# Two transformer blocks with a 16-of-16384 expert layer: decode of expert indices moved to GpSimd and ScalarE, order of work beside the gathers changed

## The chip, the cores and the metric

The kernel runs on one core of a Trainium2 chip. Its engines are TensorE (PE), VectorE (DVE), ScalarE (ACT), GpSimd (POOL) and SyncE (SP); each works through its own queue in order. The metric is the device time of one execution in microseconds, and less is better. Three timed runs of the kernel before took 2024.09, 2025.24 and 2026.83 us, median 2025.24.

## What is computed

x has 256 tokens of 1024 features. A first block (gated linear attention, a spatial gating unit, then the expert layer below) is followed by two layers of a second block, in which x attends to itself and to a second stream, ctx, of 256 tokens. ctx itself goes through attention and a gated FFN only in the first of these layers. The parts that the change touches:

```python
def peer(h, w_q, keys1, keys2, expert_down, expert_up):     # 8 heads, top 16 of 128 x 128 experts
    q = einsum('btd,dq->btq', h, w_q).reshape(B, T, 8, 2, 128)
    s1, s2 = q[..., 0, :] @ keys1.T, q[..., 1, :] @ keys2.T
    v1, i1 = top_k(s1, 16); v2, i2 = top_k(s2, 16)
    cand = v1[..., :, None] + v2[..., None, :]              # 16 x 16 sums
    cidx = i1[..., :, None] * 128 + i2[..., None, :]
    top_s, pos = top_k(cand.reshape(..., 256), 16)
    idx = take_along_axis(cidx.reshape(..., 256), pos)      # rows of the tables
    g = softmax(top_s)
    a = gelu(einsum('pd,ped->pe', h, expert_down[idx]))     # 128 rows of 1024 a token
    return einsum('pe,ped->pd', g * a, expert_up[idx])

# ctx in the first layer of the second block
o = softmax(q @ k.T * scale) @ v                            # three kinds of heads, 20 maps of 256 x 256 in all
y = (silu(h @ w_gate) * (h @ w_up)) @ w_down                # hidden width 2816 = 22 x 128
```

## The kernel before, in words

Tokens lie on the 128 partitions, in two halves t = 0 and 1. The program is written with a scheduler that orders each engine's instructions by its own model of their times, within the dependences and the extra edges that the code gives: `issue_after(ins)` puts what is traced inside it behind `ins` on the same engine. `merge` and `slow` interleave generators by the numbers that they yield, so a `yield 1.46` is meant as 1.46 us of the stage's time, and the order of writing is the scheduler's priority.

**The expert stage** (`experts`, L764) makes four passes of 128 rows. A row is one expert of each of 128 tokens, 128 x 1024 floats or 512 KiB, gathered by an indirect DMA that GpSimd issues (`gather`, L875) into a ring of 7 buffers. *Dot* passes multiply the row with h on DVE and add up (`dot_slot`, L859, instruction at L862); *up* passes add weight times row into a sum (L793, L795). h in the dot passes and the sum in the up passes lie in one PSUM tile, `side` (called h2p in the rows). The passes run dot and up for t = 0, then dot and up for t = 1; here they are called dot 0, up 0, dot 1 and up 1.

**The search** for one head and half (`winners`, L825) is some 25 short instructions on DVE: two top-16 searches over 128 scores (`top16`), the 256 sums `cand`, a top-16 over them, then the decode: the positions are split in two numbers by shift and mask (`pp`), cast on ScalarE (`ppf`, `vif`), compared with 0 to 15 to a one-hot `oh` (L849), multiplied with the found indices (L852), summed (L854) and put together to `idx` (L855). Heads of t = 0 are searched beside dot 0, one step after each row; those of t = 1 are written two steps a row from row 60 of up 0 on (`SECOND_AT`, `behind`). Between a dot and an up pass stand the softmax of the 8 heads' scores (`softmax_gate`), a gelu over all 128 dots on ScalarE (L784) and a product on DVE (L785).

**ctx's first layer** runs beside the expert stage, slowed by `CTX_SLOW` = 1.4. Its softmax (L1173) takes one score map at a time: matmul into PSUM, maximum on DVE (`sst`, L1180), exponential with its sum on ScalarE (L1182). Its norms (`norm_T`) scale the rows on DVE (L371). Its FFN goes through 22 feature tiles of 128: two weight loads and 16 matmuls into `gu`, tanh on ScalarE (L1404), two products on DVE (`fth`, L1405, and `hid`, L1413), a third load and four matmuls with `hid`, and the generator yields 6.8 and 3.4 a tile. Weight loads go out on SP's queue into four buffers `raw`; all other DMA of the stage is the gathers.

After the stage the two layers of x run alone, bound by TensorE and its operands; the ctx stream's key and value part of the second layer lies among them.

Of the kernel before, what the change touches and what calls it, by code (L numbers as in the profile page):

```python
# [20 lines left out]
P = 128  # L21
# [88 lines left out]
class Kern:  # L110
# [653 lines left out]
    def experts(self, A):  # L764

        nc, a, dot = self.nc, self.a, self.dot
# [8 lines left out]
        for t in range(2):  # L775
            for h in range(8):
                ahead = self.winners(A, h + 1, 0) if t == 0 and h < 7 else iter(())
                for n in range(16):
                    self.dot_slot(t, h * 16 + n)
                    next(ahead, None)  # L780
                    yield 1.46
                drain(ahead)
            self.softmax_gate(A, t)
            nc.scalar.activation(dot[:, t, :], dot[:, t, :], AF.Gelu)  # L784
            nc.vector.tensor_mul(dot[:, t, :], dot[:, t, :], self.gate[:, t].rearrange("p a b -> p (a b)"))  # L785
            y2 = side
            for s in range(P):
                if s >= SECOND_AT:
                    self.behind(second, 2)
                r = self.gather(a["up"], t, s)  # L790
                w = dot[:, t, s:s + 1]
                if s == 0:
                    self.slot = nc.vector.tensor_scalar(y2, r, w, None, op0=ALU.mult)  # L793
                else:
                    self.slot = nc.vector.scalar_tensor_tensor(y2, r, w, y2, op0=ALU.mult, op1=ALU.add)  # L795
# [3 lines left out]
            nc.vector.tensor_mul(g, y2, self.gate2)  # L799
# [25 lines left out]
    def winners(self, A, h, t):  # L825
# [4 lines left out]
        for f in range(2):  # L830
# [28 lines left out]
    def dot_slot(self, t, s):  # L859
# [3 lines left out]
                                       accum_out=self.dot[:, t, s:s + 1])  # L863
# [320 lines left out]

    def scale_rows(self, x, r, st, i):
# [16 lines left out]
    def attn_diff(self, st, l, W, kvs, dd):  # L1202
# [28 lines left out]
    def attn_pair(self, st, W, yT, tile_i, qf, kf, vf, kvs):  # L1231
# [87 lines left out]
    def layer(self, st, l, W, K, only_kv=False):  # L1319
# [56 lines left out]
        with ExitStack() as fs:  # L1376
# [14 lines left out]
            for ft in range(NFT):  # L1391
                if split and ft == GVFT:
                    gv = self.bcast_row(self.scratch(), cc[:, 3, :])
                with self.pinned(norm_ins):
                    self.upto(vec, VN)
# [8 lines left out]
                nc.scalar.activation(th, ps[:, 0, :], AF.Tanh, scale=0.5)  # L1404
                nc.vector.scalar_tensor_tensor(th, th, 1.0, ps[:, 0, :], op0=ALU.add, op1=ALU.mult)  # L1405
# [8 lines left out]
                yield 5.1 if split else 6.8  # L1414
# [8 lines left out]
                products(0)  # L1423
                later.append(products)
# [9 lines left out]
                yield 2.6 if split else 3.4  # L1434
# [20 lines left out]
    def run(self):  # L1455
# [10 lines left out]
        with ExitStack() as cs:  # L1466
# [9 lines left out]
            self.dot = self.ring.tile([P, 2, P], F32, name="dot", bufs=1)  # L1476
# [11 lines left out]
            merge(self.experts(A), slow(ctx_gen(), CTX_SLOW))  # L1488
# [126 lines left out]
SECOND_AT = 60  # L1615
# [37 lines left out]
```

## Time and profile before

| quantity | value |
|---|---|
| median of three runs | 2025.24 us |
| profiled execution, its own time | 2027.85 us |
| its span | 2026.1 us |
| PE / DVE / ACT / POOL busy, share of the span | 75% / 71% / 33% / 28% |
| DMA moved | 542.33 MB, mean 268 GB/s |
| expert stage, first to last row instruction's pass end | 357.0 to 1218.7 us |
| mean granted TensorE clock | 0.876 |

The page divides the span in 40 slices of 50.65 us. The shares of the whole span say little, since the stages have different limits: up to about 350 us the first block runs on TensorE, from 1219 us on the two layers of x do, and in between lie the 512 gathered rows. So the reading goes by stretches of the expert stage, its waits, and the groups of instructions that the change removes or adds. "Idle before" of a group is the time in which the engine stood still just before its instructions, with what ended it.

### The profile page before, as it was taken

How to read it: one execution, taken by the hardware profiler on the slowest of the kernel's cores; microseconds unless marked ns; L12 is line 12 of the kernel's file. 1: busy time of each engine (PE TensorE's matmuls, PEld its weight loads, DVE VectorE, ACT ScalarE, POOL GpSimd, SP SyncE). 2: the span in 40 equal slices, each digit the busy share in tenths (PEclk: the TensorE clock that was granted, in tenths of full speed). 3: DMA queues.
4: the chain of work that ended last, by engine and by line, in shares of the span. 5: the costliest groups of instructions: out<-in, count | busy, mean ns of one | idle time of the engine just before them, and what ended most of it. 6: DMA issues, size and time to landing. Idle time of an engine off the chain costs nothing.

```text
span 2026.1 us, 23153 instructions
## 1 busy us (share of the span) xinstructions
PE 1526.6 (75%) x7984; PEld 1153.7 (57%) x7984; DVE 1447.7 (71%) x2591; ACT 666.7 (33%) x1286; POOL 565.9 (28%) x596
## 2 busy tenths in 40 slices
PE   5999999995477877877000007789999988889997
PEld 1766666843344655554000006577988966769997
DVE  2444544999978799867999996664877557745554
ACT  2533333232242000000000006565544356755443
POOL 0000001555655444545776760300000004000000
PEclk9999999997568999988555558989999998899999
DMA  8867796998979999999999993423887543025652
GB/s 317 328 218 261 242 348 248 332 398 317 351 284 375 408 344 331 397 394 389 409 401 380 409 384 112 164 85 97 306 275 266 167 140 112 1 66 185 187 186 94
DMA packets 150184, 542.33 MB, mean 268 GB/s; under 512 B 16801, under 2 KB 17185, under 8 KB 150066
## 3 DMA queue, kind: packets, MB, share of 16 engines
q1 hardware_dynamic: 75152, 269.53, 38.3%
q0 software_dynamic: 73728, 268.47, 34.8%
q10 hardware_dynamic: 1186, 2.85, 0.4%
q8 instruction: 63, 1.03, 0.2%
q14 instruction: 55, 0.45, 0.1%
HBM read 539.73 MB, written 1.05 MB: 267 GB/s over the span
## 4 chain that ended last, share of the span: by engine, by line
PE 48%; DVE 24%; issue 9%; POOL 9%; DMA 8%; ACT 2%; POOLq 0%; SPq 0%; DVEq 0%; ACTq 0%
PE blk L206 14%; PE gu L206 12%; POOL row L878 7%; DVE row L862 7%; PE f L206 6%; DVE h2p L795 6%; PE ada L255 3%; DMA raw<-in_w_ada 2%; PE S L206 2%; DMA row<-in_up,idx 2%; PE po L1250 2%; PE PT L1196 2%; DMA vraw<-in_w_ada 2%; DMA araw<-in_w_ada 1%; PE qk L206 1%
## 5 line engine op out<-in xcount | busy, mean ns | idle before, releaser
L190 DVE TENSOR_TENSOR wlo<-raw,whi 128x1024 fp32r<-128x1024 f32 (+1 forms) x245 | 297.5, 1220 | 272.0 <-ACT whi L188 264.0
L188 ACT CAST whi<-raw 128x1024 fp32r<-128x1024 f32 (+1 forms) x245 | 254.3, 1043 | 329.6 <-PE blk L206 112.9
L795 DVE SCALAR_TENSOR_TENSOR h2p<-row,dot,h2p 128x1024 f32<-128x1024 f32 x254 | 326.8, 1286 | 17.4 <-DMA row<-in_up,idx 11.4
L862 DVE SCALAR_TENSOR_TENSOR row<-row,h2p 128x1024 f32<-128x1024 f32 x256 | 306.6, 1220 | 14.3 <-DMA row<-in_down,idx 11.5
L878 POOL DMA_INDIRECT row<-in_down,idx x256 | 245.5, 959 | 197.2 <-DVE row L862 118.5
L878 POOL DMA_INDIRECT row<-in_up,idx x256 | 243.1, 949 | 187.9 <-DVE h2p L795 103.3
L379 PE MATMUL nT<-cst,w 128*128 128x128 f32 x112 | 20.5, 341 | 293.8 <-DVE ss L305 270.6
L307 POOL TENSOR_TENSOR ss<-ss,mhalf 128x1 f32<-128x1 f32 (+1 forms) x39 | 25.4, 655 | 711.8 <-DVE ss L305 709.7
L206 PE MATMUL gu<-bTh,whi 128*128 128x256 f32 x704 | 201.0, 286 | 3.3 <-ACT bTh L352 2.8
L206 PE MATMUL gu<-bTl,whi 128*128 128x256 f32 x704 | 201.0, 285 | 0.7 <-DVE bTl L357 0.7
L206 PE MATMUL gu<-bTh,wlo 128*128 128x256 f32 x704 | 200.6, 285 | 0.1
L379 PEld LDWEIGHTS nT<-cst,w 128*128 128x128 f32 x112 | 16.4, 175 | 299.3 <-ACT junk L326 271.4
L206 PE MATMUL gu<-bT,raw 128*128 128x256 f32 x704 | 157.0, 381 | 0.7 <-DMA raw<-in_wgu 0.7
L206 PEld LDWEIGHTS gu<-bT,raw 128*128 128x128 f32 x704 | 134.6, 191 | 28.7 <-issue 10.4
L206 PEld LDWEIGHTS gu<-bTh,whi 128*128 128x128 f32 x704 | 135.9, 193 | 6.2 <-ACT bTh L352 3.4
L206 PEld LDWEIGHTS gu<-bTl,whi 128*128 128x128 f32 x704 | 136.0, 193 | 3.1 <-DVE bTl L357 1.5
L206 PEld LDWEIGHTS gu<-bTh,wlo 128*128 128x128 f32 x704 | 136.0, 193 | 1.6 <-DVE wlo L190 0.3
L206 PE MATMUL f<-raw,hid 128*128 128x512 f32 x176 | 93.2, 679 | 55.4 <-DVE hid L1413 51.6
L206 PEld LDWEIGHTS f<-raw,hid 128*128 128x128 f32 x176 | 36.1, 216 | 102.4 <-DVE hid L1413 63.8
L1180 DVE TENSOR_REDUCE sst<-S 128x1 f32<-128x512 f32 (+1 forms) x120 | 70.4, 601 | 32.4 <-PE S L206 31.5
L206 PE MATMUL blk<-wlo,hTh 128*128 128x512 f32 x224 | 90.8, 405 | 0.0
L206 PE MATMUL blk<-whi,hTl 128*128 128x512 f32 x224 | 88.1, 396 | 0.0
(406 smaller groups left out, 3102.0 us busy)
## 6 DMA issues: line engine op xcount, KB each, us to landing
raw<-in_wgu SPq DMA_DIRECT2D x132, 512.0 KB, 4.6
araw<-in_w_ada SPq DMA_DIRECT2D x72, 512.0 KB, 6.1
raw<-in_wd SPq DMA_DIRECT2D x66, 512.0 KB, 5.0
raw<-in_w1b SPq DMA_DIRECT2D x56, 512.0 KB, 5.1
raw<-in_w_ada SPq DMA_DIRECT2D x40, 512.0 KB, 4.4
vraw<-in_w_ada SPq DMA_DIRECT2D x32, 512.0 KB, 5.2
raw<-in_w2c SPq DMA_DIRECT2D x24, 512.0 KB, 4.8
raw<-in_w2o SPq DMA_DIRECT2D x24, 512.0 KB, 4.0
```

The costliest lines, as they stand in the source:

```text
L188: nc.scalar.copy(hi[:, :n], raw[:, :n])
L190: nc.vector.tensor_sub(lo[:, :n], raw[:, :n], hi[:, :n].bitcast(F32))
L206: self.mm_last = self.nc.tensor.matmul(out, l, r, start=first and i == 0, stop=last and i == n - 1)
L255: mm = nc.tensor.matmul(ps[32 * j:32 * j + 32, :], lhs[:, k, :], raws[j // 2][:, j % 2 * 512:(j % 2 + 1) * 512], start=k == 0, stop=k == K ...
L307: nc.gpsimd.tensor_tensor(ss, ss, self.mhalf[:, :n], op=ALU.pow)
L379: nc.tensor.transpose(ps[:, q, t * P:(t + 1) * P], xn[t][:, k * P:(k + 1) * P], self.ident)
L795: self.slot = nc.vector.scalar_tensor_tensor(y2, r, w, y2, op0=ALU.mult, op1=ALU.add)
L862: self.slot = nc.vector.scalar_tensor_tensor(r, r, 1.0, self.side, op0=ALU.mult, op1=ALU.mult, accum_out=self.dot[:, t, s:s + 1])
L878: nc.gpsimd.indirect_dma_start(out=r, out_offset=None, in_=table, in_offset=bass.IndirectOffsetOnAxis(ap=self.idx[:, t, s:s + 1], axis=0))
L1180: nc.vector.tensor_reduce(st[:, 0:1], ps, axis=AX.X, op=ALU.max, negate=True)
L1196: nc.tensor.transpose(ps[:, j, :], pr[:, j * P:(j + 1) * P], self.ident)
L1250: nc.tensor.matmul(po[64 * i:64 * i + 64, :], vf(kvs[j // 2], j % 2, i), PTs[i][:, j, :], start=j == 0, stop=j == 2 * nk - 1)
```

## The change

- **Decode.** For every head but the first of t = 0, the one-hot is made without DVE: GpSimd subtracts, ScalarE takes Abs and then Relu(1 - x), GpSimd multiplies. DVE keeps the sum and the last step. `winners` gets three more steps.
- **Searches of t = 1.** One step behind two of every three rows, from row 1 of up 0, instead of two steps behind each row from row 60. What is left is written after the pass.
- **Gelu in two parts.** The dots lie in tiles of 96 and 32 (`FIRST`); the first is weighed at row 116 of the dot pass, the second at row 4 of the up pass, and the softmax over heads' scores is written before the eighth head's rows.
- **ctx's softmax in pairs.** Where there is one key source, two score maps share a PSUM tile and one maximum instruction of 128x2x256; a yield of `CTX_LAG` = 2.0 stands before what uses them.
- **ctx's FFN.** The gate and up products of a tile are written before the DVE products of the tile ahead of it, and the yields are 9.0 and 5.6 a tile (x 1.4 = 20.4, that is 14 rows of 1.46).
- **ctx's norms** scale on ScalarE. All of ctx's generator is pinned behind the latest row instruction (`rows_first`).

```diff
+            if len(op) == 2:
+                self.xn_ins = nc.vector.tensor_scalar(j, x[:, t, :], r, None, op0=ALU.mult)
+            else:
+                nc.scalar.activation(j, x[:, t, :], AF.Copy, scale=r)
...
+                if h == 7:
+                    self.softmax_gate(A, t)
                 for n in range(16):
                     self.dot_slot(t, h * 16 + n)
                     next(ahead, None)
+                    if h * 16 + n == FIRST + 20:
+                        self.weigh(t, 0)
...
             for s in range(P):
-                if s >= SECOND_AT:
-                    self.behind(second, 2)
+                if t == 0 and s % 3:
+                    self.behind(second, 1)
...
+                if s == 4:
+                    self.weigh(t, 1)
...
+    def rows_first(self, g):
+        while True:
+            with self.pinned(self.slot):
+                y = next(g, None)
...
+        if h == 0 and t == 0:
+            nc.vector.tensor_tensor(oh, pb, ib, op=ALU.is_equal)
+            nc.vector.tensor_tensor(oh, oh, vb, op=ALU.mult)
+        else:
+            yield
+            nc.gpsimd.tensor_tensor(oh, pb, ib, op=ALU.subtract)
+            nc.scalar.activation(oh, oh, AF.Abs)
+            nc.scalar.activation(oh, oh, AF.Relu, scale=-1.0, bias=1.0)
+            yield
+            yield
+            nc.gpsimd.tensor_tensor(oh, oh, vb, op=ALU.mult)
...
+    def softmax2(self, W, pairs):
+        ps = self._ps(self.acc, [P, 2, T], "acc", "S")
+        for i, (lhs, kT) in enumerate(pairs):
+            self.mm(ps[:, i, :], self.pairs(lhs, kT), True, True)
+        nc.vector.tensor_reduce(st[:, 0:2], ps, axis=AX.X, op=ALU.max, negate=True)
+        for i in range(2):
+            nc.scalar.activation(pr[i], ps[:, i, :], AF.Exp, bias=st[:, i:i + 1], accum_out=st[:, 2 + i:3 + i])
...
+                for ft in range(NFT + 1):
+                    this = front(ft) if ft < NFT else None
+                    yield FRONT
+                    if ahead is not None:
+                        down(ft - 1, hidden(*ahead))(1)
+                        yield BACK
+                    ahead = this
...
+            self.slot = None
+            merge(self.experts(A), slow(self.rows_first(ctx_gen()), CTX_SLOW))
...
-SECOND_AT = 60
+FIRST = 96
+CTX_LAG = 2.0
+FRONT = 9.0
+BACK = 5.6
```

What the built programs show, at three places. GpSimd at the start of dot 0, before (`DMA row` is a gather, `ss` a norm's power function):

```order
L878 DMA row<-in_down,idx 128x1024 x2
L307 TENSOR_TENSOR ss_2702<-ss_2702,mhalf 128x1
L307 TENSOR_TENSOR ss_2709<-ss_2709,mhalf 128x1
L878 DMA row<-in_down,idx 128x1024 x42
L307 TENSOR_TENSOR ss<-ss,mhalf 128x2
```

and after:

```order
L916 DMA row<-in_down,idx 128x1024 x8
L884 TENSOR_TENSOR oh<-ppf,iota 128x512
L916 DMA row<-in_down,idx 128x1024 x2
L889 TENSOR_TENSOR oh<-oh,vif 128x512
L916 DMA row<-in_down,idx 128x1024 x6
L884 TENSOR_TENSOR oh<-ppf,iota 128x512
L916 DMA row<-in_down,idx 128x1024
```

The decode's difference and product now stand in the gathers' queue, one or two gathers apart, at 15 places of the stage.

ScalarE in up 0, where the FFN's tanh (`fth`) and the decode's casts meet, before:

```order
L1404 ACTIVATE fth<-gu 128x256 x4
L845 CAST vif<-tvi 128x32
L1404 ACTIVATE fth<-gu 128x256
L844 CAST ppf<-pp 128x32
L845 CAST vif<-tvi 128x32
```

and after:

```order
L1468 ACTIVATE fth<-gu 128x256
L870 CAST ppf<-pp 128x32
L1468 ACTIVATE fth<-gu 128x256
L885 ACTIVATE oh<-oh 128x512
L886 ACTIVATE oh<-oh 128x512
L1468 ACTIVATE fth<-gu 128x256
L871 CAST vif<-tvi 128x32
```

Abs and Relu (L885, L886) stand behind a tanh in this queue; the row shown is the first head of t = 1 that meets the FFN.

DVE where feature tiles pass among rows, before (up 0):

```order
L1405 SCALAR_TENSOR_TENSOR fth<-fth,gu 128x256
L1413 SCALAR_TENSOR_TENSOR hid<-fth,gu 128x256
L795 SCALAR_TENSOR_TENSOR h2p<-row,dot,h2p 128x1024 x6
L1405 SCALAR_TENSOR_TENSOR fth<-fth,gu 128x256
L1413 SCALAR_TENSOR_TENSOR hid<-fth,gu 128x256
```

and after (dot 1):

```order
L1473 SCALAR_TENSOR_TENSOR fth<-fth,gu 128x256
L900 SCALAR_TENSOR_TENSOR row,dot_2262<-row,h2p 128x1024
L1481 SCALAR_TENSOR_TENSOR hid<-fth,gu 128x256
L900 SCALAR_TENSOR_TENSOR row,dot_2262<-row,h2p 128x1024 x13
L1473 SCALAR_TENSOR_TENSOR fth<-fth,gu 128x256
```

Tiles that stood 6 rows apart on DVE at the start of the FFN now stand 14 apart. In the order before, the 22 tiles lie in up 0 (14) and dot 1 (8); after, in up 0 (8), dot 1 (9) and up 1 (5, the last ahead of its row 82).

## Rows read from the trace of the kernel before

**Rows 1.** Passes: length, busy of PE, PEld, DVE, ACT, POOL; clock, DMA, GB/s.

```profile
357.00:583.50 226.50, 161.53 (x603) 107.11 (x601) 221.61 (x589) 65.95 (x194) 130.36 (x134) 0.77 0.95 353
583.50:846.00 262.50, 215.91 (x786) 143.10 (x785) 232.16 (x443) 38.63 (x108) 124.35 (x132) 0.91 0.94 352
846.00:1048.40 202.40, 86.98 (x298) 58.52 (x296) 167.70 (x289) 10.90 (x23) 123.45 (x131) 0.74 1.01 399
1048.40:1218.70 170.30, 0.00 (x0) 0.00 (x0) 165.08 (x129) 0.00 (x0) 115.01 (x122) 0.50 0.98 383
```

**Rows 2.** The same columns: dot rows alone, and a stretch in dot 0.

```profile
985.00:1026.00 41.00, 0.00 (x0) 0.00 (x0) 38.84 (x63) 0.00 (x0) 29.91 (x32) 0.50 1.03 410
480.00:560.00 80.00, 38.30 (x134) 27.04 (x134) 80.00 (x189) 22.58 (x71) 50.56 (x54) 0.54 0.94 336
```

**Rows 3.** DVE's row instructions, 347 to 1219 us: busy, mean ns | idle before.

```profile
L862 DVE SCALAR_TENSOR_TENSOR row<-row,h2p 128x1024 f32<-128x1024 f32 x256 | 306.6, 1220 | 14.3 <-DMA row<-in_down,idx 11.5
L795 DVE SCALAR_TENSOR_TENSOR h2p<-row,dot,h2p 128x1024 f32<-128x1024 f32 x254 | 326.8, 1286 | 17.4 <-DMA row<-in_up,idx 11.4 <-DVE h2p L795 0.2
```

**Rows 4.** DVE's waits in dot 0, up 0, dot 1: total us, times, longest.

```profile
DVE sst L1180 <- PE S L206: 4.1, 4, 1.9
DVE h2p L795 <- DMA row<-in_up,idx: 10.9, 12, 2.3
DVE fth L1405 <- ACT fth L1404: 10.5, 5, 3.3
DVE fth L1405 <- ACT fth L1404: 20.0, 6, 5.4
```

**Rows 5.** More DVE groups, columns as in rows 3.

```profile
L849 DVE TENSOR_TENSOR oh<-ppf,iota 128x512 bf16<-128x512 bf16 x15 | 10.2, 683 | 0.0
L852 DVE TENSOR_TENSOR oh<-oh,vif 128x512 bf16<-128x512 bf16 x15 | 6.2, 415 | 0.0
L1180 DVE TENSOR_REDUCE sst<-S 128x1 f32<-128x256 f32 x40 | 16.5, 429 | 9.7 <-PE S L206 9.5
L1405 DVE SCALAR_TENSOR_TENSOR fth<-fth,gu 128x256 f32<-128x256 f32 x22 | 9.1, 414 | 30.5 <-ACT fth L1404 30.5
L371 DVE TENSOR_SCALAR w<-cx,ss 128x1024 f32<-128x1024 f32 x4 | 3.0, 753 | 3.6 <-POOL ss L307 3.5
```

**Rows 6.** One line on two engines: count, ns min/median/max, first, last start.

```profile
L980 POOL TENSOR_TENSOR qB<-qB,gqs x4: 1279/1290/1528, 1270.0 to 1690.0; 128x512 f32<-128x512 f32 x4
L980 DVE TENSOR_TENSOR qB<-qB,gqs x2: 675/675/675, 450.9 to 453.6; 128x512 f32<-128x512 f32 x2
```

**Rows 7.** ScalarE's groups, 347 to 1219 us, columns as in rows 3.

```profile
L1404 ACT ACTIVATE fth<-gu 128x256 f32<-128x256 f32 x22 | 8.4, 383 | 186.5 <-PE gu L206 186.5
L976 ACT ACTIVATE w<-qB 128x512 f32<-128x512 f32 x2 | 1.3, 630 | 0.1
```

**Rows 8.** DVE and GpSimd in time, a later layer: start us, us, instruction.

```profile
1274.95 0.21 DVE L1216 SCALAR_TENSOR_TENSOR nls<-nls,sst,nlam 128x1 f32<-128x1 f32 x1
1278.27 0.69 DVE L357 TENSOR_TENSOR kmTxl<-tr,kmTxh 96x512 fp32r<-96x512 f32 x1
1281.94 1.16 DVE L1216 SCALAR_TENSOR_TENSOR nls<-nls,sst,nlam 128x1 f32<-128x1 f32 x1
1278.07 0.72 POOL L933 TENSOR_TENSOR w<-qB,cst 128x256 f32<-128x256 f32 x1
1281.79 2.53 POOL L937 TENSOR_TENSOR qB<-qB,cst 128x512 f32<-128x512 f32 x2
```

**Rows 9.** DVE's groups over the whole span, columns as in rows 3.

```profile
L1180 DVE TENSOR_REDUCE sst<-S 128x1 f32<-128x512 f32 x80 | 53.9, 687 | 22.8 <-PE S L206 21.9
```

**Rows 10.** Gathers of the up passes, from issue to landing.

```profile
DMA to landing us min/median/max: 4.1/6.4/14.5
```

**Rows 11.** TensorE's groups over the whole span, columns as in rows 3.

```profile
L206 PE MATMUL gu<-bT,raw 128*128 128x256 f32 x704 | 157.0, 381 | 0.7 <-DMA raw<-in_wgu 0.7
L206 PE MATMUL f<-raw,hid 128*128 128x512 f32 x176 | 93.2, 679 | 55.4 <-DVE hid L1413 51.6 <-DMA raw<-in_wd 3.7
```

More of the change, by code (lines that the diff above doesn't have):

```diff
@@ L764, in experts @@
     def experts(self, A):
-        nc, a, dot = self.nc, self.a, self.dot
+        nc, a = self.nc, self.a
         self.side = side = self.px.tile([P, D], F32, name="h2p")
@@ L798, in experts @@
             g = self.ring.tile([P, D], F32, tag="y2", name="y2", bufs=1)
-            nc.vector.tensor_mul(g, y2, self.gate2)
+            nc.vector.tensor_mul(g, side, self.gate2)
             if t == 0:
@@ L804, in experts, with at, weigh @@
             nc.vector.scalar_tensor_tensor(self.xt[:, t, :], self.xt[:, t, :], r, self.fin, op0=ALU.mult, op1=ALU.mult)
+    def at(self, t, s):
+        p = int(s >= FIRST)
+        return self.dots[t, p][:, s - p * FIRST:s - p * FIRST + 1]
+    def weigh(self, t, p):
+        d = self.dots[t, p]
+        n = d.shape[1]
+        self.nc.scalar.activation(d, d, AF.Gelu)
+        self.nc.vector.tensor_mul(d, d, self.gate[:, t].rearrange("p a b -> p (a b)")[:, p * FIRST:p * FIRST + n])
     def behind(self, g, n):
@@ L862, in dot_slot @@
         self.slot = nc.vector.scalar_tensor_tensor(r, r, 1.0, self.side, op0=ALU.mult, op1=ALU.mult,
-                                       accum_out=self.dot[:, t, s:s + 1])
+                                       accum_out=self.at(t, s))
     def top16(self, v, vi, x):
@@ L1210, in attn_diff @@
                 qs = slice(qt * P, (qt + 1) * P)
-                (p0, s0), (p1, s1) = [self.softmax(W, (qdS[:, 2 * h + s, qs],), [(k["kdS"][:, 2 * h + s, :],) for k in kvs], nk)
-                                      for s in range(2)]
+                if nk == 1:
+                    (p0, p1), ss = self.softmax2(W, [((qdS[:, 2 * h + s, qs],), (kvs[0]["kdS"][:, 2 * h + s, :],)) for s in range(2)])
+                    s0, s1 = ss[:, 0:1], ss[:, 1:2]
+                    yield CTX_LAG
+                else:
+                    (p0, s0), (p1, s1) = [self.softmax(W, (qdS[:, 2 * h + s, qs],), [(k["kdS"][:, 2 * h + s, :],) for k in kvs], nk)
+                                          for s in range(2)]
                 c = self.small.tile([P, 2], F32, tag="nls", name="nls", bufs=6)
@@ L1238, in attn_pair @@
             PTs.append(PT)
+            if nk == 1:
+                prs, s = self.softmax2(W, [(self.sl(qf(i), lambda z: z[:, qt * P:(qt + 1) * P]), kf(kvs[0], i)) for qt in range(2)])
+                yield CTX_LAG
+                r = self.small.tile([P, 2], F32, tag="rs2", name="rs", bufs=6)
+                nc.vector.reciprocal(r, s)
+                for qt in range(2):
+                    self.scale_rows(prs[qt], r[:, qt:qt + 1], st, 2 * i + qt)
+                    self.probT(prs[qt], PT, qt, nk, True)
+                yield 2.0
+                continue
             for qt in range(2):
@@ L1390, in layer, with front @@
                               for g in (1, 2)])
[L1391 to L1395, printed above, removed]
+            def front(ft):
                 ps = self.pst([P, 2, T], "gu")
@@ L1423, in layer @@
                 products(0)
+                return products
+            if not split:
+                ahead = None
+                for ft in range(NFT + 1):
[5 more added lines that the diff above has]
+                    ahead = this
+            for ft in range(NFT if split else 0):
+                if ft == GVFT:
+                    gv = self.bcast_row(self.scratch(), cc[:, 3, :])
+                with self.pinned(norm_ins):
+                    self.upto(vec, VN)
+                hid = hidden(*front(ft))
+                yield 5.1
+                products = down(ft, hid)
                 later.append(products)
@@ L1433, in layer @@
                         next(side[0], None)
-                yield 2.6 if split else 3.4
+                yield 2.6
             drain(vec)
@@ L1475, in run @@
             self.ring = self.pool(cs, "ring", RING)
-            self.dot = self.ring.tile([P, 2, P], F32, name="dot", bufs=1)
+            self.dots = {(t, p): self.ring.tile([P, (FIRST, P - FIRST)[p]], F32, name=f"dot{t}{p}", bufs=1)
+                         for t in range(2) for p in range(2)}
             A = self.pool(cs, "T")
```

31 lines of the change are left out of this document (18 added, 13 removed).

## The prediction

> **What bounds the kernel now.** I read the page's forty slices first: in the middle of the span its DMA line stands near full without a break, while before and after it does not. This is the expert stage, 512 gathered rows of 512 KiB (524,288 bytes) with ctx's layer beside them, and nearly all of the change lies in it. I then cut it at the first DVE instruction of each of its four passes of 128 rows [rows 1]: **dot 0** takes 226.5 us, **up 0** 262.5, **dot 1** 202.4 and **up 1** 170.3, together 861.7 us of a span of 2026.1. Two resources are nearly full in all of it: DVE is busy for 786.6 us, and the four rates times their lengths give 80.0 + 92.4 + 80.8 + 65.2 = 318.3 MB, or 369 GB/s.
>
> What each can do at best shows where rows stand alone. At 985 to 1026 us 32 dot rows move in 41 us (1.28 us a row) at 410 GB/s with a DMA share of 1.03 [rows 2], while DVE's own work is 1.22 us a row [rows 3]: there the transfers set the pace. In up 1 DVE does: 170.3 / 128 = 1.33 us a row against 1.286 of busy time [rows 1, 3], so rows that follow each other cost 5.2 us of small gaps in 128. The stage's floors are then 318.3 MB at 410 GB/s = 776 us, and some 807 us of DVE (786.6 and four times 5.2). Dot 0 is DVE's (221.6 of 226.5 busy). Up 0 is the worst: 30.3 us idle and only 352 GB/s. Dot 1 is the transfers' (399 GB/s, share 1.01), its 34.7 us of idle DVE notwithstanding. The named waits of DVE [rows 4] are 30.5 us for ctx's tanh (10.5 in up 0, 20.0 in dot 1), 10.9 in up 0 for rows that had not landed and, in dot 0, 4.1 for ctx's scores.
>
> On the transfers a page speaks against any gain: the Trainium skill, "DMA: Bandwidth & Descriptors", Specifications, has an HBM limit of about 358 GB/s a core, by which 318.3 MB would need 889 us. The trace shows 399 GB/s over 202 us and 410 over 41 [rows 1, 2], so the measurement decides, and the sum goes by these two.
>
> **The change, part by part.** *Decode.* 15 of the 16 heads lose two DVE instructions of 0.683 and 0.415 us [rows 5], 1.10 a head. GpSimd gets two of 128x512 for each; the nearest rows are 1.28 to 1.53 us there, where DVE takes 0.675 on the same line [rows 6]: 30 x 1.3 = 39 us on a queue busy for 493 of 862 us. ScalarE gets 30 x 0.63 = 19 us [rows 7] on 115 busy. Idle time covers both. What is queued behind them matters more: on GpSimd every gather stands behind the product, which waits for ScalarE's Relu, and one or two gathers (29.91 us for 32, 0.93 each [rows 2]) stand between difference and product. With ScalarE free that chain is two ACTIVATEs, 1.3 us, so the queue stands still for under half a microsecond; I cost it at 0, and the other end is a rival below. The reduce on DVE stands several rows later, and I cost its wait at 0 too (at most 1 us x 15).
>
> *Contention.* In a later layer a DVE instruction with both inputs in SBUF took 1.16 us as GpSimd worked on 128x512 operands, and 0.21 some 7 us earlier, while one that reads PSUM took 0.69 with GpSimd at work as well [rows 8]. Row instructions read one input (side) from PSUM, so they are of the second kind; the candidates' sum and the last index step are of the first, two a head. I take 0; the bound is 30 x 1.3 = 39 us.
>
> *Paired softmax.* Two reduces of 0.429 become one of 128x512, 0.687 [rows 5, 9]: 0.17 us x 20; fewer reciprocals are left out of the sum. The lag is meant to take the waits for scores. *Norm on ScalarE.* Four instructions of 0.75 leave DVE in this stage [rows 5]; two of them stand before row 0, in the first gather's flight. The later layer's kv part moves two more, beside TensorE's work: 0, at most 2 us either way. *Gelu in parts.* Two more table loads on an idle ScalarE, and the weights of up 0's first rows are ready earlier: 0.
>
> *Searches spread, FFN slowed.* By the order, 14 feature tiles stand in up 0 and 8 in dot 1 before; afterwards 8 in up 0, 9 in dot 1 and 5 in up 1, up to its row 82. A tile is three loads of 524,288 bytes, 1.57 MB, and two DVE instructions of 0.414, 0.83 us [rows 5]. About 1.5 of the second half's eight heads slip from up 0 into dot 1. A head's price is bounded by what is left of up 0: 232.2 - 128 x 1.286 - 14 x 0.83 - 2.6 (six reduces) - 1.5 (norm) = 52 us for eight heads and ctx's rest, so at most 6.5 a head, 5.4 without decode, and 8 for the 1.5.
>
> The sum, pass by pass:
> - Dot 0, DVE-bound: 226.5 - 7 x 1.10 (7.7) - 17 pairs x 0.17 (2.9) - 4.1 (scores) + 3 pairs that come over from up 0 (2.1) = 214.
> - Up 0: 232.2 busy - 8.8 (decode) - 8 (1.5 heads) - 5.0 (six tiles) - 2.6 (six reduces) - 1.5 (norm) = 206.3, and 5.2 of gaps: 211. Transfers: 92.4 - 6 x 1.57 = 83.0 MB, 202 us at 410 and 208 at 399. With two limits this close neither is met in full; I take 216, between that floor and 243 (first rival).
> - Dot 1, transfers: one tile more, and about as much of the next layer's first weights less, so 202.4 at 399 GB/s and 197 at 410: 201. Its 20 us of tanh waits buy nothing, since the transfers were full meanwhile.
> - Up 1 now pays: 82 rows (43.0 MB), 5 tiles (7.9) and the weights just named (1.6) are 52.5 MB, 131.5 us at 399, and 46 rows alone take 61.2 us: 193 against 170.3.
>
> 214 + 216 + 201 + 193 = 824, 38 us less than 861.7. The profiled execution took 2027.85 us around its span of 2026.1; the median of the three timed runs is 2025.24. Nothing outside the stage moves, so 2025.24 - 38 = **1987 us**. Its own range runs from 209 + 211 + 197 + 188 = 805 (-57, about 1966 with the norm's 2 us) to 2010.
>
> **Rivals.** *Pushed on, not saved* (2016 us). If up 0 is held by the ring of 7 rows (median flight 6.4 us [rows 10]) and not by work, fewer weights there bring nothing: it falls by DVE work removed alone, 8.8 + 5.0 + 2.6 + 1.5 = 17.9 and the gaps' share, to about 243, while up 1 pays its 23: 214 + 243 + 202 + 193 = 852, -10. For it: DVE waited for rows in 10.9 us of up 0. Against it: only a third of its idle time is that, and dot 1 moves 399 GB/s with the same ring.
>
> *GpSimd held by ScalarE* (2065 us, slower). ScalarE works in order and waits for TensorE for 186.5 / 22 = 8.5 us a tile before its tanh [rows 7]. If a head's Abs stands behind such a wait, the product waits, and no gather is issued. A row's lead is 7 x 216 / 128 = 11.8 us less a flight of 6.4 and the issue of 0.93: 4.5. The eight heads among the FFN would lose 8 x (8.5 - 4.5) = 32, still -6 in all. But TensorE's work thins as well: a tile is (157.0 + 93.2) / 22 = 11.4 us of it [rows 11], and where TensorE was busy for half the time (480 to 560 us) the granted clock was 0.54, near its lower level of 1.2 GHz [rows 2]. The gate and up products then take 14.3 us a tile instead of 7.1, an estimate by doubling, and a hold of that length costs 8 x 9.8 = 78: 40 us slower. It decides from a hold of 4.5 + 38 / 8 = 9.3 us a head. Against it: before, DVE's own decode stood behind the same casts on ScalarE and idled 0.0 us for them [rows 5].
>
> *Ports* (2026 us, the same). Every GpSimd instruction delays DVE by its whole length: 39 us, the gain. The Trainium skill, "Advanced Engine Details and Errata", GPSIMD Details, says that the two engines share a read and a write interface and conflict where DVE runs in a 2-port mode or has two SBUF inputs. By that rule the rows are spared and two short instructions a head are exposed; the trace agrees with both halves (1.16 against 0.21, and 0.69 under GpSimd's work), hence the small chance.
>
> *Better than the range* (1960 us): up 0 and dot 1 both run at 410 GB/s and dot 0 loses more.
>
> **How the numbers follow.** Forecast 0.68, pushed on 0.12, held 0.10, ports 0.05, better 0.05. The range reaches from 1966 over pushed on to 2022 and leaves out the held case, ports and the better one. A measurement of this kernel can tell about 0.2%, 4 us, from no change. Faster: 0.68 + 0.05 + 0.10 of pushed on = 0.83. Same: 0.02 of it and 0.04 of ports, 0.06. Slower: held and the rest of ports, 0.11.
>
> **What would show it.** Cut the new trace at the same four places: about 214, 216, 201 and 193 us. Up 1 must be longer than 170 and dot 1 unchanged; if up 0 stays above 240, pushed on is right. DVE's waits for tanh should be near 0, and the largest left should be for rows. GpSimd's idle time before the product, with ScalarE's Relu as releaser, should be under 15 us in all; above 70 it is the held case, with the clock near 0.5 through the FFN. Row instructions longer than 1.22 and 1.286 us, or candidate sums much longer than before, mean ports. The base is wrong if the stretch before row 0 or after row 511 changes by over 3 us.

## The result and the profile after

The changed kernel takes 2005.1 us (median of 7 runs, 2001.9 to 2015.5) where the kernel before takes 2026.4 in the same runs: a ratio of 0.990, 95% interval 0.987 to 0.993, or 21 us less. The forecast was 1987 us, 38 less, with a range of 1966 to 2022. So the sign and the range held, and the gain was put nearly twice too high.

The four passes of the changed kernel, cut at the same places as in [rows 1] (start and end, length, busy time of PE, PEld, DVE, ACT and POOL with their counts, granted clock, DMA share, GB/s):

```profile
359.10:582.20 223.10, 164.20 (x645) 110.08 (x644) 219.17 (x561) 82.91 (x235) 143.45 (x147) 0.79 0.94 347
582.20:806.80 224.60, 148.37 (x510) 94.70 (x509) 210.46 (x369) 38.33 (x90) 138.33 (x146) 0.79 1.00 387
806.80:1008.20 201.40, 114.16 (x361) 74.74 (x360) 167.63 (x307) 9.40 (x20) 124.68 (x132) 0.77 1.00 396
1008.20:1199.60 191.40, 61.76 (x176) 37.31 (x174) 174.96 (x152) 6.97 (x16) 119.83 (x124) 0.66 0.98 387
```

Against 226.5, 262.5, 202.4 and 170.3 these are -3.4, -37.9, -1.0 and +21.1: 840.5 for 861.7, together -21.2. Dot 1 (201 forecast) and up 1 (193) came as worked out. Dot 0 (214) and up 0 (216) are 9 us each too long, and they make the whole miss.

VectorE's largest waits in dot 0, up 0 and dot 1 of the changed kernel (total us, times, longest), beside [rows 4]:

```profile
DVE qgTl L357 <- ACT qgTh L352: 1.7, 1, 1.7
DVE rr L1015 <- ACT w L1014: 0.8, 1, 0.8
DVE row L900 <- DMA row<-in_down,idx: 0.7, 1, 0.7
...
DVE h2p L798 <- DMA row<-in_up,idx: 6.8, 10, 1.2
DVE w L1375 <- ACT junk L1374: 2.6, 3, 1.7
DVE rs L1300 <- ACT prob L1234: 2.3, 1, 2.3
...
DVE row L900 <- DMA row<-in_down,idx: 30.6, 38, 1.4
```

The tanh (`fth`) is in none of them: 30.5 us of waiting are gone. In dot 1 the 20.0 us for it and the 11.5 us for rows of before became 30.6 us for rows, and the pass is as long as before. The decode's and the pairs' groups over the stage (busy us, mean ns, idle time before them and what ended it), beside [rows 5]:

```profile
L889 POOL TENSOR_TENSOR oh<-oh,vif 128x512 bf16<-128x512 bf16 x15 | 17.4, 1157 | 1.7 <-ACT oh L886 1.5
...
L884 POOL TENSOR_TENSOR oh<-ppf,iota 128x512 bf16<-128x512 bf16 x15 | 15.8, 1051 | 1.9 <-ACT ppf L870 1.7
L1230 DVE TENSOR_REDUCE sst<-S 128x2 f32<-128x512 f32 x20 | 13.5, 687 | 0.2 <-PE S L206 0.2
```

GpSimd's product waited 1.5 us for ScalarE in all 15 heads, so the rival in which ScalarE holds the gathers is out; its 33.2 us are below the 39 assumed.

### The profile page after: what moved, and what is told of

Its sections match the earlier page's. It is cut to its first block, busy times and chain, and to the rows that moved or that the text cites. A ratio compares the mean times of both kernels' runs of the same rounds, so it can differ in the third digit from the quotient of the medians.

```text
span 2000.7 us, 23149 instructions
## 1 busy us (share of the span) xinstructions
PE 1545.3 (77%) x7984; PEld 1156.4 (58%) x7984; DVE 1429.2 (71%) x2525; ACT 692.7 (35%) x1326; POOL 598.5 (30%) x626
## 3 DMA queue, kind: packets, MB, share of 16 engines
HBM read 539.73 MB, written 1.05 MB: 270 GB/s over the span
## 4 chain that ended last, share of the span: by engine, by line
PE 47%; DVE 19%; DMA 14%; POOL 9%; issue 8%; ACT 2%; SPq 0%; POOLq 0%; DVEq 0%; ACTq 0%
PE blk L206 16%; PE gu L206 12%; POOL row L916 7%; DVE row L900 6%; DMA row<-in_up,idx 6%; PE f L206 6%; DVE h2p L798 5%; PE ada L255 3%; DMA raw<-in_w_ada 2%; DMA row<-in_down,idx 2%; PE S L206 2%; PE po L1317 2%; PE PT L1248 1%; DMA araw<-in_w_ada 1%; PE qk L206 1%
## 5 line engine op out<-in xcount | busy, mean ns | idle before, releaser
L190 DVE TENSOR_TENSOR wlo<-raw,whi 128x1024 fp32r<-128x1024 f32 (+1 forms) x245 | 297.5, 1220 | 276.7 <-ACT whi L188 266.5
L798 DVE SCALAR_TENSOR_TENSOR h2p<-row,dot,h2p 128x1024 f32<-128x1024 f32 x254 | 326.8, 1286 | 24.5 <-DMA row<-in_up,idx 19.7
L900 DVE SCALAR_TENSOR_TENSOR row<-row,h2p 128x1024 f32<-128x1024 f32 x256 | 308.6, 1220 | 33.9 <-DMA row<-in_down,idx 31.4
L206 PE MATMUL f<-raw,hid 128*128 128x512 f32 x176 | 130.1, 907 | 201.6 <-DVE hid L1481 201.6
L206 PEld LDWEIGHTS f<-raw,hid 128*128 128x128 f32 x176 | 50.0, 299 | 271.6 <-DVE hid L1481 210.4
L206 PE MATMUL gu<-bTh,whi 128*128 128x256 f32 x704 | 201.0, 285 | 4.9 <-ACT bTh L352 2.8
L206 PE MATMUL gu<-bTl,whi 128*128 128x256 f32 x704 | 201.0, 286 | 0.7 <-DVE bTl L357 0.7
L1468 ACT ACTIVATE fth<-gu 128x256 f32<-128x256 f32 x66 | 25.1, 380 | 321.8 <-PE gu L206 321.8
L206 PE MATMUL blk<-raw,bT 128*128 128x512 f32 (+1 forms) x192 | 86.4, 600 | 0.0
```

Source lines behind the costliest of these rows:

```text
L190: nc.vector.tensor_sub(lo[:, :n], raw[:, :n], hi[:, :n].bitcast(F32))
L206: self.mm_last = self.nc.tensor.matmul(out, l, r, start=first and i == 0, stop=last and i == n - 1)
L798: self.slot = nc.vector.scalar_tensor_tensor(side, r, w, side, op0=ALU.mult, op1=ALU.add)
L900: self.slot = nc.vector.scalar_tensor_tensor(r, r, 1.0, self.side, op0=ALU.mult, op1=ALU.mult, accum_out=self.at(t, s))
```

## The experiments

Each kernel is the changed one or the one before with the edit that is named. The table gives for each the ratio to the kernel before, run beside it, with its 95% interval, the four passes of its profile (cut at the first row instruction of each), their sum, and the time before row 0 and after row 511.

| kernel | ratio | dot 0, up 0, dot 1, up 1 | sum | before, after |
|---|---|---|---|---|
| before | 1 | 226.5, 262.5, 202.4, 170.3 | 861.7 | 357.0, 807.4 |
| changed | 0.990 (0.987 to 0.993) | 223.1, 224.6, 201.4, 191.4 | 840.5 | 359.1, 801.1 |
| e1 decode on DVE, fewer steps | 0.994 (0.992 to 0.996) | 224.1, 235.4, 199.1, 190.9 | 849.5 | 356.7, 809.2 |
| e5 decode on DVE, same steps | 0.992 (0.990 to 0.995) | 222.6, 233.8, 201.0, 192.0 | 849.4 | 361.6, 802.4 |
| e4 before, decode alone | 0.996 (0.994 to 0.998) | 235.6, 249.4, 204.1, 169.7 | 858.8 | 361.9, 800.5 |
| e6 five differences | 1.002 (1.000 to 1.005) | 235.1, 233.0, 203.8, 191.7 | 863.6 | 361.7, 806.1 |
| e7 no pairs | 0.992 (0.989 to 0.995) | 226.5, 226.2, 202.9, 190.1 | 845.7 | 358.0, 814.5 |
| e2 old pace | 0.986 (0.983 to 0.989) | 224.2, 230.9, 209.9, 169.6 | 834.6 | 357.0, 801.1 |
| e8 no pipeline | 0.987 (0.984 to 0.990) | 224.2, 226.5, 199.5, 188.3 | 838.5 | 362.2, 803.9 |
| b3 old pace, no pipeline | 0.989 (0.986 to 0.992) | 223.6, 236.5, 209.1, 169.6 | 838.8 | 358.6, 800.1 |
| e9 rows not first | 0.991 (0.987 to 0.994) | 229.2, 258.3, 185.3, 169.8 | 842.6 | 361.0, 803.2 |
| e10 before, rows first | 0.998 (0.995 to 1.000) | 226.6, 263.0, 202.3, 169.8 | 861.7 | 356.3, 806.8 |
| b1 heads in dot 1 | 0.990 (0.988 to 0.993) | 223.3, 225.8, 205.8, 191.5 | 846.4 | 358.4, 805.4 |
| b2 heads and slow ctx | 0.991 (0.987 to 0.994) | 216.1, 215.6, 217.7, 195.4 | 844.8 | 359.2, 805.8 |

The last column varies by 5 and 13 us among kernels whose code there is the same (changed, e2, e7, e8), so the tail's -6.3 us in the changed kernel can't be put down to the change, and a single profile's span is worth less than its passes. The passes are from one profile each. Their sums and the ratios tell the same to about 5 us (e4, at the worst, is 2.9 us faster than before by its passes and 8.3 by its ratio), so a difference below that is not settled by either alone.

**Decode.** e1 puts `if True:` for `if h == 0 and t == 0:`; that also drops three steps, so that eight heads stand in up 0 for six. e5 keeps the steps:

```diff
-            nc.gpsimd.tensor_tensor(oh, pb, ib, op=ALU.subtract)
-            nc.scalar.activation(oh, oh, AF.Abs)
-            nc.scalar.activation(oh, oh, AF.Relu, scale=-1.0, bias=1.0)
+            nc.vector.tensor_tensor(oh, pb, ib, op=ALU.is_equal)
...
-            nc.gpsimd.tensor_tensor(oh, oh, vb, op=ALU.mult)
+            nc.vector.tensor_tensor(oh, oh, vb, op=ALU.mult)
```

> The changed kernel with the decode of all 16 heads back on VectorE (two instructions a head, as before). Theory: in the profiles the two instructions cost VectorE 0.93 us a head from end to end (6.54 us for seven heads of dot 0), and GpSimd's share lengthens a few VectorE copies in dot 0 by 0.7 us each, 2.6 us in all. So dot 0 gets 6.5 - 2.6 = 4 us longer (227), up 0 with its six heads 5 (230), dot 1 and up 1 stay at 201 and 191: 9 us slower than the changed kernel, about 2014. Rival (the decode is worth nothing, because what it frees is lost to the shared port or to other waits): the same as the changed kernel within 3 us, dot 0 at 223.

> The changed kernel with the decode of 15 heads on VectorE again, at the same steps as GpSimd had it, so that six heads stay in up 0 (with the decode moved back and its steps left out, as in the earlier run, eight stood there). Theory: the earlier run's 8.7 us are decode and spread together. In dot 0 the decode gives nothing (6.5 us of VectorE less, 2.6 lost on copies that GpSimd holds up, 2.8 in other waits); in up 0 six heads cost 6 x 0.93 = 5.6 us of VectorE, of which the transfers, nearly full, hide half. So 2 to 5 us slower than the changed kernel, up 0 at 227 to 230. Rival (the decode alone is worth the whole): 8 to 10 us slower, up 0 at 235.

Both sums are 9 us longer than the changed kernel's, e5's by 8.9, its ratio by 0.3%, 6 us, though the intervals of the two ratios overlap. So the decode is worth some 6 to 9 of the 21 us, and the two heads more in up 0 nothing (235.4 and 199.1 against 233.8 and 201.0: two microseconds moved). For e1 the theory's total holds, its split doesn't. Of e5 the rival is right by the passes: all of it lies in up 0, and dot 0 does not change; its ratio lies between the two. In up 0 of e5 (its window, then its waits) VectorE has 6.9 us more to do and the transfers fall to 372 GB/s:

```profile
584.20:818.10 233.90, 158.14 (x563) 102.21 (x564) 217.39 (x389) 41.36 (x111) 126.27 (x134) 0.82 0.97 372
...
DVE rs L1298 <- ACT prob L1232: 4.0, 5, 1.5
...
DVE sst L1228 <- PE S L206: 1.0, 1, 1.0
```

The waits show the other half of it: with more work on VectorE two of ctx's 20 pairs slip out of dot 0 into up 0, and wait there for scores and exponentials. So dot 0 of e5 does less, and its unchanged length doesn't price the decode there alone.

e4 puts the new decode alone into the kernel before.

> The kernel before with the new decode alone (GpSimd and ScalarE, 15 heads). Theory: dot 0 loses 6.5 us and gets 2.6 back from the copies that GpSimd holds up, up 0 loses 8 x 0.93 = 7 us of VectorE, of which waits for rows and for tanh may eat half: 8 us faster than before, between 4 and 11. Rival (ports or queue: the decode's gain is lost again): the same as before within 3 us.

The ratio says 8 us, the passes only 3 (235.6 + 249.4 against 226.5 + 262.5: work moved from up 0 to dot 0). Faster, as the theory had it; how much of it belongs to the decode, this run does not tell.

**Contention.** In dot 0 of the changed kernel three VectorE groups are longer than before; first the kernel before, then the changed one:

```profile
L992 DVE TENSOR_TENSOR w<-w,w 128x256 fp32r<-128x256 f32 x2 | 0.8, 423 | 0.0
L1055 DVE COPY w<-kA 128x128 f32<-128x128 f32 x2 | 0.3, 214 | 0.0
L817 DVE COPY mx<-gate 128x8 f32<-128x8 f32 x1 | 0.2, 157 | 0.0
```

```profile
L1030 DVE TENSOR_TENSOR w<-w,w 128x256 fp32r<-128x256 f32 x2 | 1.5, 767 | 0.0
L1093 DVE COPY w<-kA 128x128 f32<-128x128 f32 x2 | 1.1, 574 | 0.0
L843 DVE COPY mx<-gate 128x8 f32<-128x8 f32 x1 | 0.9, 924 | 0.0
```

That is 2.2 us, all of it in three instructions that run beside one of GpSimd's `oh` instructions (the copy into `mx` at 450.09 us takes 0.92 beside one from 449.83 to 450.98). e6 repeats GpSimd's difference, `for _ in range(5):`, in front of the unchanged rest.

> The changed kernel with GpSimd's difference computed five times over (60 more instructions of 128x512, 1.05 us each, the output is the same). Theory: a GpSimd instruction costs VectorE only where it overlaps one of a few kinds, copies and products from SBUF to SBUF, 0.7 us each time; 14 of them in dot 0 hit four. With 42 some 8 to 12 are hit, dot 0 gets 3 to 6 us longer; the gathers stand 4.2 us longer behind each head's difference, which a row's lead (9 to 14 us against a flight of 6 to 9) mostly covers: 4 to 12 us slower than the changed kernel in all. Rival (every GpSimd instruction holds VectorE up by its length): 60 x 1.05, over 50 us slower. Second rival (neither counts): within 2 us, no VectorE instruction longer.

It costs 23.1 us in the passes (26 by the ratios), 0.39 for each of the 60 instructions: more than the theory's 4 to 12, far less than their own length, so both rivals are out as well. In time, VectorE then GpSimd (start us, us):

```profile
401.17 1.46 DVE L866 TENSOR_SCALAR pp<-pos 128x16 uint32<-128x16 uint32 x1
402.55 0.16 DVE L867 TENSOR_SCALAR pp<-pos 128x16 uint32<-128x16 uint32 x1
402.63 0.41 DVE L859 TENSOR_TENSOR cand<-tv 128x256 f32<-128x256 f32 x1
...
401.44 1.16 POOL L890 TENSOR_TENSOR oh<-oh,vif 128x512 bf16<-128x512 bf16 x1
```

A shift of 16 elements, which takes 0.17 us in the kernel before, lasts until GpSimd's instruction ends (402.60), though its record begins 0.27 us before that one's; the mask behind it takes 0.16. Beside GpSimd's `oh` instructions, 14 of VectorE's in dot 0 are each over 0.3 us longer than the same instruction in e5, which has no such work on GpSimd; VectorE is busy there for 228.2 us against 219.2 in the changed kernel. The row instructions are not among them:

```profile
L798 DVE SCALAR_TENSOR_TENSOR h2p<-row,dot,h2p 128x1024 f32<-128x1024 f32 x254 | 326.1, 1284 | 24.2 <-DMA row<-in_up,idx 19.7
L901 DVE SCALAR_TENSOR_TENSOR row<-row,h2p 128x1024 f32<-128x1024 f32 x256 | 306.2, 1211 | 30.9 <-DMA row<-in_down,idx 28.6
...
L893 DVE TENSOR_REDUCE ix<-oh 128x32 f32<-128x512 bf16 x15 | 10.2, 679 | 15.8 <-POOL oh L890 15.8
```

The other half of e6's cost is the last row: VectorE waits 15.8 us for the product (9.7 of them in up 0, which is 8.4 us longer), 0.5 in the changed kernel. The decode's chain was just covered, and 4 us more of it are not.

**Pairs.** e7 takes the old branch of both softmax places (`if False:` for `if nk == 1:`).

> The changed kernel with ctx's softmax undone: two scores, two reduces of 128x256 and no lag, as before (40 reduces in dot 0 for 20). Theory: a pair saves 2 x 0.345 - 0.607 = 0.083 us from end to end, 1.7 in all, and the waits for scores come back in dot 0, where the kernel before has 4.1 us; they were half replaced by others, so dot 0 gets 3 to 6 us longer (226 to 229) and the rest stays. Rival (the waits are filled by whatever comes next, the pairs are worth nothing): dot 0 within 1 us of 223.

Dot 0 is 226.5, 3.4 longer, as the theory had it, and the sum 5.2 longer. But the named waits for scores are only 0.7 us there, with 4.5 us at four other places. VectorE is busy for 1.9 us more (221.0 against 219.2, with 40 reduces of 128x256 for 20 pairs), and all its named waits are 5.2 us against 3.7.

**The FFN's place.** Four runs move the tiles. e2 sets `FRONT, BACK = 6.8, 3.4`; e8 runs `hidden(*front(ft))` in one piece at the new pace; b3 does both; e9 merges `slow(ctx_gen(), CTX_SLOW)` without `rows_first`. e10 puts `rows_first` alone into the kernel before.

> The changed kernel with ctx's FFN at the old pace (6.8 + 3.4 for 9.0 + 5.6), its software pipeline kept. The order then has 11 feature tiles in up 0, 11 in dot 1 and none in up 1 (8, 9 and 5 in the changed kernel). Theory (what leaves up 0 is paid in up 1, the transfers decide): up 0 gets 3 tiles, 4.7 MB, and goes from 224.6 to about 231; dot 1 gets 2, 3.1 MB, and goes from 201 to 209; up 1 falls from 191 to 170. Sum 833, 7 us faster than the changed kernel or the same. Rival (the slow pace is what saves): up 0 rises by more than 20 us, towards the 262 of before, and waits for tanh come back (30 us before): 5 to 20 us slower than the changed kernel.

> The changed kernel with ctx's FFN at the new pace but each tile's tanh and hidden part again ahead of the next tile's products (no software pipeline). Theory (transfers are full in up 0, dot 1 and the first part of up 1, share 0.97 to 1.03): VectorE's waits for tanh may come back by some us, and cost nothing, for rows are late anyway: the same as the changed kernel within 3 us, passes 223, 224 to 227, 201, 191. Rival (the pipeline is what brought up 0 down): the 10.5 us of tanh waits of before come back in up 0 as time, 8 us slower or more.

> The changed kernel with the FFN's part of the change taken back, its pace (6.8 + 3.4) and its pipeline; decode, spread searches, pairs, gelu in two parts, norm on ScalarE and the rule of rows first stay. By the order 12 tiles in up 0, 10 in dot 1, none in up 1. Theory: the transfers decide, as with the old pace alone (passes 224, 231, 210, 170, sum 834.6), and the pipeline is worth nothing: 224 + 233 + 206 + 170 = 833, 7 us faster than the changed kernel. Rival (at the fast pace the pipeline is needed): tanh waits come back, 9.5 rows a tile being shorter than TensorE's work, and the sum is 840 or more.

> The changed kernel without the rule that puts every instruction of ctx's layer behind the latest row's. By the order VectorE then has 18 feature tiles in up 0, 4 in dot 1 and none in up 1 (8, 9 and 5 with it). Theory (this rule is what takes the tanh waits away, since the pipeline's undoing brought none back): waits for tanh return as 0.75 to 2.5 us a tile, up 0 goes beyond 255, dot 1 falls to 185 to 190 and up 1 to 170; the sum of the passes is 850 or more, 10 us or more slower than the changed kernel. Rival (only the transfers count): 10 tiles more are 15.7 MB, 39 us in up 0, and 20 and 21 us come back in dot 1 and up 1: the sum stays at 835 to 842.

> The kernel before with that rule alone (ctx's instructions behind the latest row's), all else as before; 12 tiles in up 0 and 10 in dot 1. Theory: the 30 us of tanh waits of before (10.5 in up 0, 20.0 in dot 1) go to nearly nothing; in up 0 this is time, with two tiles less 10 to 15 us, in dot 1 it is not, since its transfers were full, and the two tiles more cost 8 there: sum of passes 848 to 858, 4 to 13 us faster than before. Rival (the waits turn into waits for rows): the same as before within 4 us.

e2 came out pass by pass as worked out from transfers. Its last three passes:

```profile
581.30:812.20 230.90, 182.62 (x667) 121.96 (x665) 212.68 (x368) 39.51 (x93) 138.52 (x146) 0.90 1.01 397
812.20:1022.10 209.90, 116.56 (x376) 75.96 (x376) 177.30 (x333) 14.62 (x34) 127.68 (x134) 0.79 1.01 396
1022.10:1191.70 169.60, 0.00 (x0) 0.00 (x0) 165.16 (x130) 0.21 (x1) 115.61 (x122) 0.50 0.99 389
```

All three run at a share of 0.99 to 1.01. Five tiles less in up 1 give back 21.8 us, three more in up 0 cost 6.3 and two in dot 1 8.5. The tiles in up 1 thus cost 7 us more than they save elsewhere. The slow pace is no gain: without it the kernel is the fastest of all here, 1998.7 us (0.986; its passes are 5.9 us shorter than the changed kernel's, though the two intervals overlap). e8 is as the theory says, within 3 us in the passes. b3 is not faster than e8 or e2 but also not slower than the changed kernel: its sum, 838.8, lies between the 833 of the theory and the 840 of the rival, and tanh waits of 11.3 us came back in up 0 and dot 1 (first line: waits for rows):

```profile
DVE row L900 <- DMA row<-in_down,idx: 26.6, 34, 1.8
DVE fth L1473 <- ACT fth L1468: 11.3, 6, 3.6
```

In e9 my theory fell. Ten tiles more in up 0 took 33.7 us, five less in dot 1 and in up 1 gave 16.1 and 21.6, dot 0 is 6.1 longer, and the sum is 842.6, 2 us from the changed kernel's and 0.6 above the rival's range. Up 0 and dot 1, then their waits:

```profile
590.20:848.40 258.20, 231.63 (x892) 162.63 (x890) 219.43 (x390) 42.67 (x101) 139.35 (x145) 0.96 1.01 394
848.40:1033.80 185.40, 42.92 (x136) 27.40 (x136) 173.71 (x310) 12.26 (x27) 130.07 (x134) 0.61 1.00 389
...
DVE h2p L798 <- DMA row<-in_up,idx: 25.1, 39, 2.1
...
DVE fth L1473 <- ACT fth L1468: 4.2, 4, 3.0
```

Up 0 is nearly as long as before the change (262.5), but full: 394 GB/s against 352. The waits for tanh are 4.2 us, where the theory had at least 0.75 a tile. By its passes e10's theory fell too. With the rule alone the tanh waits of dot 1 go from 20.0 us to none and waits for rows take their place (28.4 us there for 11.5), those of up 0 stay (11.3 us for 10.5), and not one pass moves by more than 0.6 us; its ratio leaves 1 to 9 us open. What keeps tanh waits away is the slow pace or the pipeline, either of them: 1.4 us in e8 and 0.4 in up 0 of e2, 11.3 where both are gone (b3).

**More work out of VectorE.** b1 takes a step of the searches behind every third row and gives five heads to dot 1:

```diff
-                    next(ahead, None)
+                    next(ahead if t == 0 else second, None)
...
-                if t == 0 and s % 3:
+                if t == 0 and s % 3 == 0:
...
-            drain(second)
```

b2 adds `CTX_SLOW = 2.2`, `FRONT = 4.33` and `BACK = 2.16`.

> The changed kernel with the second half's searches spread further: one step behind every third row of up 0 instead of two of three (three heads there), and the other five heads one step a row in dot 1. Theory (up 0 is VectorE's, dot 1 the transfers', with 34 us of idle VectorE): about 3.4 heads of 5.3 us leave up 0, 18 us of VectorE, so it falls to its transfers, 86.9 MB at 405 GB/s, 214 us; dot 1 stays at 201 to 204. 8 to 11 us faster than the changed kernel. Rival (up 0 is held by the ring of rows in flight, not by VectorE's work): up 0 stays above 222 and the whole is the same within 3 us, or slower if dot 1 grows by the searches.

> The changed kernel with the searches spread over up 0 and dot 1 (three heads and five), ctx's layer slowed from 1.4 to 2.2 and the FFN's tiles at the old 9.8 rows each. By the order 15 of ctx's 20 pairs stand in dot 0 (20 before), 5 pairs and 3 tiles in up 0, 13 tiles in dot 1 and 6 in up 1. Theory (dot 0 is VectorE's at 347 GB/s, all else the transfers' at about 397): work leaves VectorE where it is full. Dot 0 loses some 14 us of VectorE, 205 to 210; up 0 carries 80 MB, 200 to 205; dot 1 87.5 MB, 221; up 1 some 195: about 824, 16 us faster than the changed kernel and 8 faster than with the old pace alone. Rival (what leaves dot 0 and up 0 is paid in full in dot 1 and up 1): 835 to 841, no faster than the old pace alone.

In their times both rivals are right, though b2's sum lies even above its rival's range. Of b1, up 0, one stretch of 16 rows in it, and a long wait of VectorE and of GpSimd just before it (start us, us, instruction, idle time before it):

```profile
581.70:807.50 225.80, 147.54 (x510) 94.39 (x510) 197.35 (x295) 34.12 (x79) 131.30 (x139) 0.82 0.99 386
616.80:642.90 26.10, 13.25 (x70) 11.10 (x70) 24.83 (x34) 12.73 (x23) 19.20 (x21) 0.74 0.80 265
...
613.50 0.69 DVE L1374 TENSOR_TENSOR w<-blk,w 128x512 f32<-128x512 f32 x1 [5.26 <-ACT junk L1373]
618.36 0.95 POOL L915 DMA_INDIRECT row<-in_up,idx  x1 [9.31 <-DVE ss L305]
```

In b1 13.1 us of VectorE leave up 0 (210.5 to 197.4) and the pass stays. Seven of its eight stretches of 16 rows run at 392 to 411 GB/s, so there the transfers hold it. The eighth is the one shown. VectorE stood still for 5.3 us for ScalarE, at a product of ctx's block (`w`) that the order has ahead of the rows, freed no buffer meanwhile, and GpSimd issued no gather for 9.3 us (the `ss` that its wait names stands right behind the next row). At 399 GB/s the stretch would have been 26.1 x (1 - 265 / 399) = 8.8 us shorter, an estimate, which is about the 8 to 11 us that the theory promised. The same wait is at most 1.7 us long in the changed kernel.

Up 0 of b2:

```profile
575.30:791.00 215.70, 109.29 (x384) 67.42 (x383) 198.97 (x305) 46.65 (x116) 132.74 (x140) 0.70 0.97 366
```

In b2 dot 0 and up 0 are 16 us shorter and the last two passes 20 longer; up 0 is bound by neither side in full, 366 GB/s with VectorE busy for 199 of 216 us.

## Why the forecast was right in sign and too large

**Right.** Dot 1 is the transfers' and its tanh waits buy nothing (201.4). Up 1 pays for the tiles (191.4). The largest waits left are for rows, GpSimd's product hardly waits, and the rows keep their length. *Pushed on* (243 in up 0), *held* (2065) and *ports* as the loss of the whole gain did not come. The prediction's sign of a wrong base, over 3 us of change after row 511, did appear, but that stretch takes 800 to 815 us in the eleven kernels with the new code there and 800 to 807 in the three with the old.

**Dot 0, 9 us short.** Four terms of its sum were mis-sized, none was of the wrong kind.
- Decode, 7.7: adjacent records overlap by 0.08 us (in the lines of e6, 402.55 + 0.16 against a next start at 402.63), so two instructions less free 1.10 - 0.16 = 0.94 us a head, 6.6.
- Pairs, 2.9: one record less, and 0.08 of overlap less with it, is 0.09 a pair, 1.5; the three pairs that came over cost 1.8 instead of 2.1.
- Score waits, 4.1: they fell to 0.2, but waits for `qgTh`, `w`, rows and `pd` of 3.5 us stand in their place.
- Contention, 0: 2.2 us on the three groups above. The prediction counted two instructions a head with both inputs in SBUF as exposed; copies and a scalar shift are exposed too.

Together -6.6 - 1.5 + 1.8 - 0.4 + 2.2 = -4.5, and -3.4 was measured; dot 0 varies by about as much among kernels with the same code there (223.1 to 224.2: changed, e2, e8, b1). In e5 dot 0 is no longer with the decode back, but two pairs have left it.

**Up 0, 9 us short.** The step that failed is the 83.0 MB. The queues of up 0, first before, then after the change (q0 the rows, q1 the weights: packets, MB, share):

```profile
q0 software_dynamic: 18030, 65.68, 67.0%
q1 hardware_dynamic: 7289, 26.58, 26.8%
```

```profile
q0 software_dynamic: 18951, 69.01, 79.2%
q1 hardware_dynamic: 4896, 17.83, 20.4%
```

The weights fell by 8.7 MB, about as forecast (9.4), but the rows rose by 3.3: six rows more. The kernel before had fetched most of them while it was still in dot 0 (69.18 MB of rows there, 66.74 after the change) and then stood still for ctx's scores (5.5 us): 146 GB/s in the first 16.5 us of its up 0. At 399 GB/s they are 8.3 us, nearly the whole miss. With 86.9 MB the term would have been 218 at 399, and b1's up 0, with 87.2 MB and far less VectorE work, comes to about this floor once its one held stretch is taken off (225.8 - 8.8 = 217, an estimate). The other 6.6 us are the loss of two near limits, for which the forecast had put 5 to 8. Four of its eight stretches of 16 rows:

```profile
582.20:613.30 31.10, 30.68 (x110) 14.77 (x109) 26.46 (x49) 13.07 (x36) 17.58 (x19) 1.00 1.02 407
613.30:641.90 28.60, 17.79 (x85) 13.81 (x84) 27.88 (x50) 12.28 (x23) 18.16 (x20) 0.76 0.92 335
...
749.70:775.00 25.30, 13.16 (x40) 8.46 (x40) 24.80 (x48) 2.05 (x5) 16.73 (x19) 0.70 1.03 409
775.00:806.80 31.80, 15.49 (x42) 9.47 (x43) 30.45 (x61) 3.27 (x8) 18.17 (x19) 0.66 0.97 372
```

The first and third run at full rate (in the third VectorE is busy for 98% as well), in the second and fourth VectorE is busy for 97 and 96% and the rate drops to 335 and 372. This fits a pass that costs the sum of the larger limit of each stretch, not the larger of its two sums, as only seven rows can lie between gathers and VectorE; no run changed the ring, so that reason is argued and not shown.

**What carried the gain.** By the passes, the decode gave 9 of the 21 us and the pairs with their lag 5 (6 and 4 by the ratios, whose intervals overlap the changed kernel's). Taking back the pace (e2) or the rule of rows first (e9) moves 22 to 38 us between passes and -5.9 and +2.1 in the sum; pace and pipeline together (b3) move 22 and -1.7. So the tiles' place gained nothing: the five in up 1 cost there at least what they save elsewhere. Some 7 us are not pinned to a part: the spread of the searches, the norm on ScalarE and gelu in two parts were not taken back alone.

## What to carry to other kernels

When one pass is full of transfers and the next of an engine's work, moving work between them shows as large changes in both and as nothing in the sum: add the passes up before believing either. Take the bytes of a window from its queues on both sides of the change, prefetched rows included, and count what removed instructions free from start to start, not by their recorded lengths. An instruction moved to GpSimd lengthened copies, scalar operations and products of VectorE that happened to run beside it, so put a price on it from the trace rather than zero. And when taking work off an engine leaves a pass as long as it was, look for one long wait before calling the other side the limit: in b1 a 5.3 us wait ahead of the rows cost about as much as the work taken off VectorE could have given (8.8 us, an estimate).

## What the runs showed of the hardware

GpSimd's 128x512 bf16 instructions took 1.05 and 1.16 us. Beside them, VectorE's COPY of 128x8 took 0.92 for 0.16 us, its shift of 128x16 integers 1.46 for 0.17, while in e6 the searches' MAX8 of 128x128 (276 ns, 277 before) and the row instructions with one input in PSUM kept their lengths (1211 and 1284 ns in e6, 1220 and 1286 before). The Trainium skill, "SBUF — State Buffer", Who interferes with whom, says that copies and tensor-scalar operations can take the port pair that VectorE shares with GpSimd, and that the one that issues later then waits to the end of the other's instruction. The lines of e6 agree on the end (402.63 and 402.60); the order of issue they don't show, as VectorE's record begins first. The prediction had used only half of this: instructions with two inputs in SBUF.
